# A hybrid decoder trunk on one core: priority of the norm roots, residual sums through PSUM, first weights and last block in parts, a 512-column down-projection

## The chip, the cores and the metric

The kernel runs on one core of one Trainium2 chip. The metric is the device time of one execution in microseconds (us), the median of repeated runs. TensorE multiplies, VectorE (DVE), ScalarE (ACT) and GpSimd (POOL) do the rest, SyncE (SP) issues the transfers.

## What is computed

Sixteen meta tokens stand before 1024 real ones: 1040 positions, 1024 features, float32. Two layers, each a mixer and a convolutional feed-forward network (FFN), and around each of these four a pre-norm, a post-norm and a residual:

```python
h = h + rmsnorm(mix, g[1])
ff = conv_ffn(rmsnorm(h, g[2]), ffn_w_up[l], ffn_conv[l], ffn_w_down[l])
h = h + rmsnorm(ff, g[3])
# conv_ffn: u = causal_dwconv(x @ w_up); gate, val = split(u); (silu(gate) * val) @ w_down
```

Layer 0 mixes with a gated linear recurrence over 8 heads (q, forget gate, value and output gate are projections of the normed input), layer 1 with a forgetting attention of 16 heads on shared keys and values. The output is h of the real tokens.

## The kernel before, in words

Features lie on partitions: 8 row tiles (kt) of 128 features by 1040 tokens. Tokens are cut into three blocks, 356, 342 and 342 columns in layer 0 (BLK_A), 342 each in layer 1 (BLK_B, from column 14). Every product of a weight and an activation is three matmuls on a high and a low part of each, in float32r (mm3s, L145, L148, L149). So every weight is loaded raw, cast by ACT to its high part (L97 or L135) and subtracted by DVE to its low part (L98, L138).

A norm's factor is not applied to the input but to the result. rstd_of turns a sum of squares into a factor for every column: small matmuls against ones (L164) sum over features, ACT takes the root (L169), DVE the reciprocal (L170) and a scaled diagonal (L175), matmuls spread it over all partitions in PSUM (L176), ACT copies it to SBUF where it is kept (L179). sumsq squares on ACT (L187) and adds on POOL (L188).

Layer 0's mixer begins with inputs(0): for each block four projections of head 0 (forget gate, output gate, values, queries) from weights w0, then norm0, then the four results are scaled. take(i) loads a block of x and splits it. For the later heads a hand-written order on TensorE (manual_schedule, weave) mixes the recurrence of one head with the projections of the next; for head 0 and for the post stages the order on every engine is made by a scheduler at build time, from a plan of costs and the priorities; high_priority(offset=OFF) moves instructions ahead in it. The engines then run their queues in that order and wait where something is late.

The last product before each post-norm (mixer_out's two, and the last chunk of an FFN's down-projection) runs through overlap: for each block eight output tiles, each evacuated by DVE (L575 for a mixer, L681 for an FFN) with high priority, squared and added; and, one tile into the next block, post of the block before. post calls rstd_of and then, for each row tile, loads the residual (L206), scales by gain and factor in place (L207), adds the residual (L208), stores (L210), splits the new stream for the next projections (L281 with a gain, L98 without) and adds up its squares for the next norm. With `then`, the first up-projections (or head 0 of the attention) run behind, block by block.

An FFN has 22 hidden tiles in seven chunks. For each chunk the hidden tiles are made (up-projection, convolution at L607 to L617, silu at L643, L644), then down adds the chunk's product to eight accumulators, per output tile and block, evacuated at L681. [...]

## Time and profile before

| | us |
|---|---|
| median of 3 runs | 2875.55 (2873.24 to 2882.78) |
| the profiled execution, its own time | 2883.05 |
| its span, first to last instruction | 2881.1 |

The profile shows one execution. A span's rows give busy time by engine; idle time before an instruction is put down to what released it. [...] Post stages lie at about 570 to 660, 1340 to 1425, 2070 to 2165 and 2830 to 2881 us.

### The profile page before, as it was taken

To read this page: it belongs to the slowest core of one execution; us is meant where nothing else is said; L and a number is where in the kernel's file an instruction comes from. 1 tells how busy PE (TensorE), PEld (TensorE's weight loads), DVE (VectorE), ACT (ScalarE), POOL (GpSimd) and SP (SyncE) were. 2 spreads that over 40 slices of the span, in tenths; PEclk is the share of its full clock that TensorE was granted. 3 is DMA by queue.
4 is the path that set the end of the run, shared out by engine and by line. 5 is a ranking of instruction groups with operands and counts; after the bars stand their busy time and mean duration, and the time that the engine had idled before them with its cause. 6 is when DMAs were issued, how large, how long until landed. Compare 5 with 4: busy or idle time off the path is not lost. (4 is left out here: it accounts for less than half of the span.)

```text
span 2881.1 us, 45581 instructions
## 1 busy us (share of the span) xinstructions
PE 2768.6 (96%) x17706; PEld 2709.2 (94%) x17706; DVE 1830.8 (64%) x3737; ACT 1258.2 (44%) x2421; POOL 369.6 (13%) x741
## 2 busy tenths in 40 slices
PE   8999999989999999999889999999989999999997
PEld 8999999989999999999789988898989999999997
DVE  5545445285655655566878888887684665565566
ACT  6445445455322322233566666666555232232232
POOL 2000000041100000004400000000240100010012
PEclk9999999999999999999899999999999999999999
DMA  4111111142211111112311111112242111121103
GB/s 132 30 38 30 38 40 49 37 125 62 66 38 52 45 52 38 44 52 67 92 45 45 45 45 45 45 45 93 70 124 59 45 52 52 30 65 39 52 30 113
DMA packets 202921, 163.14 MB, mean 57 GB/s; under 512 B 13984, under 2 KB 194128, under 8 KB 202704
## 3 DMA queue, kind: packets, MB, share of 16 engines
q1 hardware_dynamic: 202704, 160.23, 19.2%
q8 instruction: 138, 2.26, 0.3%
q14 instruction: 79, 0.65, 0.1%
HBM read 139.53 MB, written 20.66 MB: 56 GB/s over the span
## 5 line engine op out<-in xcount | busy, mean ns | idle before, releaser
L145 PE MATMUL pj<-x,wh 128*128 128x342 f32 (+1 forms) x2640 | 871.1, 330 | 12.6 <-DVE u L607 6.3
L149 PE MATMUL pj<-x,wl 128*128 128x342 f32 (+1 forms) x2640 | 849.3, 322 | 2.8 <-DVE wl L98 2.8
L148 PE MATMUL pj<-x,wh 128*128 128x342 f32 (+1 forms) x2640 | 849.3, 322 | 0.0
L145 PEld LDWEIGHTS pj<-x,wh 128*128 128x128 f32 x2640 | 500.8, 190 | 18.9 <-DVE u L607 7.2
L149 PEld LDWEIGHTS pj<-x,wl 128*128 128x128 f32 x2640 | 499.9, 189 | 3.1 <-DVE wl L98 3.1
L148 PEld LDWEIGHTS pj<-x,wh 128*128 128x128 f32 x2640 | 501.5, 190 | 0.1
L145 PE MATMUL g<-h,wh 128*128 128x342 f32 (+1 forms) x1056 | 339.0, 323 | 0.3
L149 PE MATMUL g<-h,wl 128*128 128x342 f32 (+1 forms) x1056 | 337.7, 321 | 0.4 <-DVE wl L138 0.4
L148 PE MATMUL g<-h,wh 128*128 128x342 f32 (+1 forms) x1008 | 323.8, 322 | 0.0
L97 ACT CAST wh<-raw 128x1024 fp32r<-128x1024 f32 x142 | 146.0, 1045 | 341.6 <-PE g L148 282.1
L145 PE MATMUL pj<-hnh,wh 128*128 128x356 f32 (+1 forms) x720 | 261.8, 364 | 9.3 <-ACT wh L97 7.0
L681 DVE TENSOR_TENSOR acc<-acc,g 128x342 f32<-128x342 f32 (+1 forms) x288 | 147.2, 511 | 193.6 <-PE g L149 193.4
L98 DVE TENSOR_TENSOR wl<-raw,wh 128x1024 fp32r<-128x1024 f32 x142 | 180.6, 1281 | 87.1 <-ACT wh L97 76.3
L149 PE MATMUL pj<-hnh,wl 128*128 128x356 f32 (+1 forms) x720 | 233.1, 324 | 0.8 <-DVE wl L98 0.8
L148 PE MATMUL pj<-hnl,wh 128*128 128x356 f32 (+1 forms) x720 | 232.8, 323 | 0.0
L612 ACT ACTIVATE y<-u,cw 128x342 f32<-128x342 f32 (+1 forms) x258 | 150.5, 584 | 182.6 <-DVE u L607 171.9
L188 POOL TENSOR_TENSOR acc<-acc,sq 128x342 f32<-128x342 f32 (+1 forms) x162 | 168.9, 1049 | 426.5 <-ACT sq L187 396.4
L613 DVE SCALAR_TENSOR_TENSOR y<-u,cw,y 128x342 f32<-128x342 f32 (+1 forms) x258 | 148.5, 576 | 111.4 <-ACT y L612 111.2
L607 DVE TENSOR_TENSOR u<-pj,r 128x342 f32<-128x342 f32 (+1 forms) x258 | 132.2, 513 | 114.1 <-PE pj L149 110.8
L145 PEld LDWEIGHTS g<-h,wh 128*128 128x128 f32 x1056 | 198.7, 189 | 2.5 <-ACT h L97 0.6
L149 PEld LDWEIGHTS g<-h,wl 128*128 128x128 f32 x1056 | 199.4, 189 | 0.6 <-DVE wl L138 0.6
L148 PEld LDWEIGHTS g<-h,wh 128*128 128x128 f32 x1008 | 190.6, 189 | 0.7 <-DVE h L98 0.2
(237 smaller groups left out, 4937.8 us busy)
## 6 DMA issues: line engine op xcount, KB each, us to landing
raw<-in_w_up_dram SPq DMA_DIRECT2D x84, 512.0 KB, 4.0
raw<-in_w_dn_dram SPq DMA_DIRECT2D x42, 512.0 KB, 4.7
raw<-in_w_in_dram SPq DMA_DIRECT2D x32, 512.0 KB, 4.1
raw<-in_kv_w_dram SPq DMA_DIRECT2D x16, 512.0 KB, 4.1
res<-h SPq DMA_DIRECT2D x44, 171.0 KB, 2.8
h<-mix SPq DMA_DIRECT2D x40, 171.0 KB, 2.2
cn<-csum SPq DMA_DIRECT2D x32, 171.0 KB, 3.6
raw<-in_w_oa_dram SPq DMA_DIRECT2D x8, 512.0 KB, 3.5
```

The source lines that it names most:

```text
L97: A.copy(hi, src)
L98: V.tensor_sub(lo, src, f(hi))
L145: PE.matmul(pt, wh, xh[:, sl], start=(j == 0), stop=False)
L148: PE.matmul(pt, wh, xl[:, sl], start=False, stop=False)
L149: PE.matmul(pt, wl, xh[:, sl], start=False, stop=(j == n - 1))
L188: eng.tensor_add(acc, acc, sq)
L607: V.tensor_mul(u[:, 2:], pt, r()[:, sl])
L612: A.activation(y, u[:, 2:], AF.Copy, scale=cw[:, j, 2:3])
L613: V.scalar_tensor_tensor(y, u[:, 1:n + 1], cw[:, j, 1:2], y, ALU.mult, ALU.add)
L681: V.tensor_add(acc_u[ot][:, sl], acc_u[ot][:, sl], pt)
```

## The change

Seven edits. The first two weights of head 0 (forget and output gate) are loaded, cast and subtracted in parts of 2, 3 and 3 row tiles (come), between the tiles of x, and their projections are interleaved; a copy of eps on ACT stands first. For head 0 TensorE's order is the written one, the norm of a block is cut in two around a projection, and the six PSUM banks of pj, g and po are taken in turn. In rstd_of root, reciprocal, diagonal and final copy get the high priority that evacuations have. In post the scaled product goes to a PSUM bank (po) and the addition reads it there. In layer 1's FFN the down-projections but the last run over two blocks of 512 columns, the last over blocks of 342, 340, 214 and 128. Before the last chunk the whole residual stream of layer 1 is fetched into eight units (h3), so post loads none. In the last chunk the eighth square is not added on POOL but goes to L164 as a second operand.

```diff
--- before.py
+++ after.py
@@ -1,4 +1,5 @@
 from contextlib import ExitStack
+from itertools import chain, zip_longest
 import concourse.bass as bass
 import concourse.tile as tile
@@ -47,6 +48,8 @@
 KSLACK, GSLACK, GLEAD, GL0, GL7 = 3000, 10000, 0.75, 0.5, 0.3
+COME = [0, 2, 5, 8]
 QR = 128
 SMB = {"u": 2, "y": 2, "sq": 2, "sq2": 1, "acc": 2, "rstd": 1, "res": 2}
 PSB = {"pj": 2, "g": 3, "pd": 2, "po": 1}
@@ -89,6 +92,8 @@
     V.memset(eps, EPS)
     gsb = cst.tile([P, 9, KT], F32, name="gsb")
     nc.sync.dma_start(gsb, gains)
+    A.copy(eps, eps)
     cw = cst.tile([P, 2 * FT - 1, 3], F32, name="cw")
     halos = cst.tile([P, 12, 2], F32, name="halos")
@@ -128,6 +133,21 @@
                 split(wh[:, :D], wl[:, :D], raw[:, :D])
             return lambda kt: (wh[:, kt * P:(kt + 1) * P], wl[:, kt * P:(kt + 1) * P])
+        def come(self, w, c0):
+            raw, wh, wl = self.load(lambda raw: [], "w")
+            def steps():
+                for a, b in zip(COME, COME[1:]):
+                    c = slice(a * P, b * P)
+                    nc.sync.dma_start(raw[:, c].rearrange("p (k c) -> p k c", c=P),
+                                      w[c, c0:c0 + P].rearrange("(k p) c -> p k c", p=P))
+                    yield
+                    split(wh[:, c], wl[:, c], raw[:, c])
+                    yield
+            return (lambda kt: (wh[:, kt * P:(kt + 1) * P], wl[:, kt * P:(kt + 1) * P])), steps()
         def rows(self, w, r0, n=P, name="w"):
             raw, wh, wl = self.load(lambda raw: [(raw[i:i + n, :D], w[r0:r0 + n, :]) for i in range(0, P, n)], name)
@@ -152,6 +172,14 @@
     def mm3(pt, pairs, sl):
         for _ in mm3s(pt, pairs, sl):
             pass
+    def whole(g):
+        while True:
+            try:
+                next(g)
+            except StopIteration as e:
+                return e.value
     def rstd_of(accs, r=None):
@@ -165,18 +193,23 @@
         q = sm.tile([P, 4], F32, tag="rq", name=nm("rq"), bufs=2)
         m = cs[-1].stop - cs[-1].start
         k = len(cs) - (m < QR)
-        for rows, j in ((QR, slice(0, k)), (m, slice(k, len(cs))))[:1 + (m < QR)]:
-            A.activation(q[:rows, j], pt[:rows, j], AF.Sqrt, bias=eps[:rows])
-            V.reciprocal(q[:rows, j], q[:rows, j])
-        dg = tmp("rstd", n)
+        with tc.high_priority(offset=OFF):
+            for rows, j in ((QR, slice(0, k)), (m, slice(k, len(cs))))[:1 + (m < QR)]:
+                A.activation(q[:rows, j], pt[:rows, j], AF.Sqrt, bias=eps[:rows])
+                V.reciprocal(q[:rows, j], q[:rows, j])
+            dg = tmp("rstd", n)
+            for j, c in enumerate(cs):
+                m = c.stop - c.start
+                V.tensor_scalar(dg[:m, c], ident[:m, :m], q[:m, j:j + 1], float(D), ALU.mult, ALU.mult)
+        yield
         pr = psum("pd")[:, :n]
         for j, c in enumerate(cs):
             m = c.stop - c.start
-            V.tensor_scalar(dg[:m, c], ident[:m, :m], q[:m, j:j + 1], float(D), ALU.mult, ALU.mult)
             PE.matmul(pr[:, c], ones[:m], dg[:m, c], start=True, stop=True)
         if r is None:
             return pr
-        A.copy(r, pr)
+        with tc.high_priority(offset=OFF):
+            A.copy(r, pr)
     def sumsq(acc, src, tag="sq", eng=G):
         if acc is None:
@@ -191,21 +224,21 @@
     def post(acc, m, sl, gpost, res, keep, pre=None, more=None):
         n = sl.stop - sl.start
-        r1 = rstd_of([acc])
+        r1 = whole(rstd_of(acc if isinstance(acc, list) else [acc]))
         acc = None
         for kt in range(KT):
             mk = m[kt][:, sl]
-            if more is None or kt % 4 < 2:
-                rs = tmp("res", n)
-            elif isinstance(more, int):
-                ru = unit(more, "res") if kt % 2 == 0 else ru
-                rs = ru[:, (kt % 2) * 350:][:, :n]
+            if isinstance(res, list):
+                rs = res[kt][:, sl]
             else:
-                rs = tmp(more[kt % 2], n)
-            nc.sync.dma_start(rs, res[kt][:, sl])
-            V.scalar_tensor_tensor(mk, mk, gsb[:, gpost, kt:kt + 1], r1, ALU.mult, ALU.mult)
-            V.tensor_add(mk, mk, rs)
+                rs = tmp(more[kt % 2] if more and kt % 4 > 1 else "res", n)
+                nc.sync.dma_start(rs, res[kt][:, sl])
+            t = psum("po")[:, :n]
+            V.scalar_tensor_tensor(t, mk, gsb[:, gpost, kt:kt + 1], r1, ALU.mult, ALU.mult)
+            V.tensor_add(mk, t, rs)
             dst = keep(kt, sl)
             nc.sync.dma_start(dst, mk[:, n - dst.shape[-1]:])
             if pre is not None:
@@ -213,7 +246,7 @@
                 acc = sumsq(acc, mk, "sq2")
         yield
         if pre is not None:
-            rstd_of([acc], pre[2][:, sl])
+            whole(rstd_of([acc], pre[2][:, sl]))
     def overlap(blocks, work, done, then=None):
@@ -290,9 +323,9 @@
     r0 = unit(45, "r0")
     hTv = hT.rearrange("(k p) t -> k p t", p=P)
     W = Weights([30, 31, 36, 37], [(24, 25), (26, 27), (28, 29), (42, 43)], OFF_W0)
-    def take(i):
+    def take(i, kts=range(KT)):
         sl = slice(BLK_A[i][0], BLK_A[i][0] + BLK_A[i][1])
-        for kt in range(KT):
+        for kt in kts:
             nc.sync.dma_start(x0[kt][:, sl], hTv[kt][:, sl])
             split_gain(hn[kt], x0[kt][:, sl], 0, kt, sl)
@@ -301,11 +334,18 @@
         accs = [None, None]
         for kt in range(KT):
             accs[kt % 2] = sumsq(accs[kt % 2], x0[kt][:, sl], eng=V if i == 0 and kt % 2 else G)
-        rstd_of(accs, r0[:, sl])
-    w0 = [W.cols(w_in, [D])]
-    take(0)
-    w0.extend(W.cols(w_in, [c * D]) for c in (3, 2, 0))
+        yield from rstd_of(accs, r0[:, sl])
+    w0 = []
+    for c in (1, 3):
+        w, g = W.come(w_in, c * D)
+        w0.append(w)
+        behind = [g] if c == 1 else behind + [g]
+    for a, b in zip(COME, COME[1:]):
+        for g in 2 * behind:
+            next(g)
+        take(0, range(a, b))
+    w0.extend(W.cols(w_in, [c * D]) for c in (2, 0))
     hg = cst.tile([P, KT], F32, name="hg")
     nc.sync.dma_start(hg, head_g)
     lb2 = cst.tile([P, 2, KT], F32, name="lb2")
@@ -416,15 +456,28 @@
         parts = [(1, forget_gate), (3, output_gate), (2, values), (0, queries)]
         if h == 0:
+            tags, done = ["pj", "pj", "g", "g", "g", "po"], [fn for _, fn in parts]
             for i, block in enumerate(BLK_A):
                 pts = []
-                for w, tag in zip(w0, ("pj", "pj", "g", "g")):
-                    yield from project(w, block, lambda *a: pts.append(a), tag)
-                norm0(i)
-                for (_, done), a in zip(parts, pts):
-                    done(*a)
+                gs = [project(w, block, lambda *a: pts.append(a), tags[(4 * i + j) % 6]) for j, w in enumerate(w0)]
+                yield from (x for xs in zip_longest(*gs[:2]) for x in xs) if i == 0 else chain(*gs[:2])
+                norm = norm0(i)
+                if i:
+                    next(norm)
+                yield from gs[2]
                 if i < len(BLK_A) - 1:
                     take(i + 1)
+                for _ in norm if i else [next(norm)]:
+                    pass
+                if i:
+                    for fn, a in zip(done, pts):
+                        fn(*a)
+                yield from gs[3]
+                for _ in norm:
+                    pass
+                for fn, a in list(zip(done, pts))[3 if i else 0:]:
+                    fn(*a)
             decays()
             keys()
             for t0, n in BLK_A:
@@ -537,8 +590,9 @@
             V.tensor_mul(o[:, sl], o[:, sl], rt[:, sl])
             yield 4 * n
-    for _ in inputs(0):
-        pass
+    with tc.manual_schedule(engines={mybir.EngineType.PE}):
+        for _ in inputs(0):
+            pass
     for h in range(HEADS - 1):
         with tc.manual_schedule(engines={mybir.EngineType.PE}):
             weave(recurrence(h), GCOL + GSLACK + KSLACK, inputs(h + 1), DCOL * GLEAD, -GL0 if h == 0 else 0.0)
@@ -594,7 +648,8 @@
     r1 = unit(40, "r1")
     keep = lambda j: lambda kt, sl: h_dram[j][kt][:, sl]
-    def ffn(l, blocks, x, r, WW, hid, accu, done, then=None):
+    def ffn(l, blocks, x, r, WW, hid, accu, done, then=None, dn=None, last=None, before=None):
         acc_u = [None] * KT
         ups = []
@@ -683,15 +738,22 @@
             def work(acc, ot, sl):
                 down(ot, sl)
                 with tc.high_priority(offset=OFF):
+                    if last and ot == KT - 1:
+                        sq = tmp("sq", sl.stop - sl.start)
+                        A.activation(sq, acc_u[ot][:, sl], AF.Square)
+                        return [acc, sq]
                     return sumsq(acc, acc_u[ot][:, sl])
             if ci == len(CHUNKS) - 1:
-                overlap(blocks, work, lambda acc, sl: done(acc, acc_u, sl), then)
+                if before:
+                    before()
+                overlap(last or blocks, work, lambda acc, sl: done(acc, acc_u, sl), then)
                 return
             for ot in range(KT):
                 if ci == 0:
                     acc_u[ot] = unit(accu[ot], f"acc{ot}")
-                for t0, n in blocks:
+                for t0, n in dn or blocks:
                     down(ot, slice(t0, t0 + n))
         count = {"hid": 0, "halo": 0}
@@ -1018,10 +1080,18 @@
     rest()
     WA = Weights([30, 31], [(37, 41), (42, 43)])
     pTh, pTl = unit(32, "pTh", F32R), unit(45, "pTl", F32R)
+    h3 = []
+    def fetch():
+        for kt, u in enumerate((0, 1, 2, 3, 8, 9, 10, 11)):
+            h3.append(unit(u, "h3"))
+            nc.sync.dma_start(h3[kt][:, B0:], h_dram[2][kt][:, B0:])
     first, rest = ffn(1, BLK_B, x3, lambda: r3, WU, [(4, 12), (5, 13), (6, 14), (7, 15)], [20, 21, 22, 23, 26, 27, 28, 29],
                       lambda acc, m, sl: post(
-                          acc, m, sl, 7, h_dram[2],
-                          lambda kt, sl: outv[kt][:, max(sl.start - NMETA, 0):sl.stop - NMETA], None, ("u", "y")))
+                          acc, m, sl, 7, h3, lambda kt, sl: outv[kt][:, max(sl.start - NMETA, 0):sl.stop - NMETA]),
+                      before=fetch, dn=[(16, 512), (528, 512)], last=[(16, 342), (358, 340), (698, 214), (912, P)])
     one, two = mixer_out(oload, w_ob, BLK_B, W, [26, 27, 28, 29, 20, 21, 22, 23],
                          lambda acc, m, sl: post(acc, m, sl, 5, h_dram[1], keep(2), (6, x3, r3)),
                          first)
```

## Rows read from the trace of the kernel before

**Rows 1.** The page, part 1: busy time and share of TensorE and the others.
```profile
PE 2768.6 (96%) x17706; PEld 2709.2 (94%) x17706; DVE 1830.8 (64%) x3737; ACT 1258.2 (44%) x2421; POOL 369.6 (13%) x741
```

**Rows 2.** The waits of PE over the span: total us, times, longest.
```profile
PE pd L164 <- POOL acc L188: 15.1, 12, 3.6
...
PE pd L176 <- DVE rstd L175: 9.7, 11, 3.1
```

**Rows 3.** Timeline, the start: start us, us, engine, line, operation [idle before <-releaser].
```profile
3.77 1.28 ACT L280 ACT_TABLE_LOAD   x1 [3.77 <-DMA x<-in_hT_dram]
...
7.02 0.66 PE L145 MATMUL pj<-hnh,wh 128*128 128x356 f32 x1 [7.02 <-ACT wh L97]
```

**Rows 4.** Timeline, PE at the end of head 0.
```profile
64.98 0.87 PE L176 MATMUL pd<-rstd,ones 128*128 128x128 f32 x6 [1.05 <-DVE rstd L175]
...
66.94 0.67 PE L145 MATMUL pj<-hnh,wh 128*128 128x356 f32 x1 [1.08 <-DVE s L366]
```

**Rows 5.** Windows behind the gaps: us, busy (instructions) by engine, PEclk, DMA, GB/s.
```profile
65.80:73.80 8.00, 6.92 (x27) 6.87 (x27) 2.40 (x6) 6.42 (x7) 0.00 (x0) 0.58 0.20 60
...
598.00:609.50 11.50, 11.44 (x50) 11.25 (x51) 4.52 (x14) 2.63 (x8) 3.72 (x5) 0.55 0.03 9
...
650.40:657.00 6.60, 4.37 (x17) 4.14 (x18) 5.93 (x11) 4.87 (x12) 4.33 (x7) 0.55 0.52 160
...
1366.90:1377.40 10.50, 10.39 (x46) 10.39 (x47) 3.98 (x13) 2.52 (x8) 2.86 (x4) 0.54 0.04 14
...
2096.40:2107.50 11.10, 11.02 (x48) 11.03 (x49) 3.11 (x12) 2.61 (x8) 3.69 (x5) 0.54 0.03 10
```

**Rows 6.** Timeline around three waits of L164 in the post stages.
```profile
584.12 2.31 POOL L188 TENSOR_TENSOR acc<-acc,sq 128x356 f32<-128x356 f32 x2 [0.30 <-ACT sq L187]
...
584.37 1.27 DVE L208 TENSOR_TENSOR mix<-mix,res 128x356 f32<-128x356 f32 x1
...
598.06 1.20 PE L164 MATMUL pd<-ones,acc 128*128 128x1 f32 x6 [2.42 <-POOL acc L188]
...
1367.01 1.18 PE L164 MATMUL pd<-ones,acc 128*128 128x1 f32 x5 [3.63 <-POOL acc L188]
...
2096.48 1.12 PE L164 MATMUL pd<-ones,acc 128*128 128x1 f32 x6 [2.57 <-POOL acc L188]
```

**Rows 7.** DVE by source line (ns min/median/max) and by form (busy us, mean ns).
```profile
L208 DVE TENSOR_TENSOR acc<-acc,res x24: 502/510/2206, 1348.3 to 2875.9; 128x342 f32<-128x342 f32 x20, 128x356 f32<-128x356 f32 x4
...
L207 DVE SCALAR_TENSOR_TENSOR mix<-mix,gsb,pd x48: 555/563/585, 576.6 to 2142.1; 128x342 f32<-128x342 f32 x40, 128x356 f32<-128x356 f32 x8
...
L681 DVE TENSOR_TENSOR acc<-acc,g 128x342 f32<-128x342 f32 x240 | 122.2, 509 | 158.5 <-PE g L149 158.2
```

**Rows 8.** Timeline, from a square root to TensorE, 638 to 655 us.
```profile
641.34 0.41 ACT L169 ACTIVATE rq<-pd,eps 128x2 f32<-128x2 f32 x2
...
645.06 0.21 DVE L170 RECIPROCAL rq<-rq 128x2 f32<-128x2 f32 x2
...
650.45 0.73 PE L176 MATMUL pd<-rstd,ones 86*128 86x86 f32 x2 [3.07 <-DVE rstd L175]
...
653.36 0.65 PE L145 MATMUL pj<-x,wh 128*128 128x342 f32 x1 [2.18 <-DVE u L607]
```

**Rows 9.** Timeline, PE: pitch of 342 columns (14 steps) and 470 (two).
```profile
2549.80 0.32 PE L148 MATMUL pj<-x,wh 128*128 128x342 f32 x1
...
2551.99 0.32 PE L145 MATMUL pj<-x,wh 128*128 128x342 f32 x1
...
1498.70 0.38 PE L879 MATMUL pd<-ks,qs 128*114 128x470 f32 x1
...
1499.13 0.21 PE L882 MATMUL pd<-maskb,identb 114*114 114x114 bf16 x1
```

**Rows 10.** Timeline, the tail.
```profile
2866.14 0.76 PE L164 MATMUL pd<-ones,acc 128*128 128x1 f32 x6 [2.36 <-POOL acc L188]
...
2869.23 1.05 DVE L207 SCALAR_TENSOR_TENSOR acc<-acc,gsb,pd 128x342 f32<-128x342 f32 x2 [1.14 <-PE pd L176]
```

## The prediction

> **What bounds the kernel now.** I read the page first. TensorE is busy for 96% of the span [rows 1], so the time can fall only where it idles, where its clock is low, or where it gets less work. Next, the waits of TensorE: the two norm steps head the list, the wait for GpSimd's last addition to a sum of squares (L164) and that for the scaled diagonal (L175 before L176), 15.1 and 9.7 us together [rows 2]. Then the timeline around the longest of them, and windows behind each. [...] At a mean clock of 0.55, 11.5 us lose 11.5 x 0.45 = 5.2 us. So a gap of 2.4 us costs almost 8 us, and a gap removed is worth three times its length. Last, VectorE's lines: in the post stages (the norm and residual after each mixer and each down-projection) it has no idle time, and what it does late is what the gaps wait for.
>
> **Start and head 0.** TensorE starts at 7.02, when one whole weight has been loaded and cast; ACT loads a table at 3.77, after the first tile of x has landed [rows 3]. The change loads two weights in parts of 2, 3 and 3 row tiles between the tiles of x, and ACT's table is loaded by a copy of eps that waits for nothing. Then the first two row tiles of each weight and one tile of x suffice, and the table's 1.28 us are gone: I put the first matmul at 5.0, a gain of 2.0. The order of TensorE is now written out. The normalisation of a block is split by a projection, so that the roots run beside 24 matmuls; at the end of head 0 this covers gaps of 1.05 and 1.08 us [rows 4], and with them the low clock from 65.8 to 73.8, 8.0 x 0.42 = 3.4 us [rows 5]. At most 2.0 + 2.1 + 3.4 = 7.5. Against it: SP issues more and smaller transfers, and in a fixed order whatever is late stops everything behind it on TensorE; the matmuls of L164 stand before the third or fourth projection and wait for the additions on GpSimd. If one block waits as long as the worst of rows 2, 3.6 us, and loses nothing in clock, the part is worth 3.9 less. From a loss of 2 to a gain of 7.5; I take **-6**, near the upper end, since the squares of a block are ready one projection ahead.
>
> **Residual sums through PSUM.** Now L207 scales in place and L208 adds the residual, both from SBUF. At 584.37 one L208 takes 1.27 us, while GpSimd works from 584.12 on [rows 6]; undisturbed it takes 0.51, at worst 2.2 [rows 7]. L207, which has one operand in PSUM, never takes more than 0.585 in 48 [rows 7]. With the product in PSUM, L208 has one SBUF operand too and should stay near the 0.51 that L681 takes with an operand in PSUM [rows 7]. An output in PSUM is shown by no DVE row; I bound it by 0.5 and 1.0 (twice L207) and take L207's own 0.56. In a block, five such additions stand in a row, so VectorE gains 5 x (1.27 - 0.51) = 3.8 us before the gap at 598.06, which is 2.42 [rows 6]. Two more places have this shape: 3.63 at 1367.01 and 2.57 at 2096.48. With the low clock behind them (5.2, 4.8 and 5.1 [rows 5]) the three hold 8.6 + 5.2 + 4.8 + 5.1 = 23.7 us.
>
> I do not take all of it. The splits behind the residual (L281, and L98 after the FFN) still read two SBUF tensors beside GpSimd, and L98 is a plain tensor_tensor like L208. And there is one PSUM bank for t, so L207 and L208 must alternate where now two of each run back to back at about 0.5 [rows 10]. I take the gaps at 598 and 2096 as halved with half of their clock, and the middle one as staying: (2.4 + 2.6 + 5.2 + 5.1) / 2 = 7.7, and 1.3 for the shorter posts elsewhere: **-9**, bounds -21 and 0.
>
> [...] The rows show an addition from PSUM as fast as one from SBUF [rows 7]. [...]
>
> **Roots ahead of the evacuations.** The square roots of a block end at 641.75 (641.34 + 0.41), but its reciprocal runs at 645.06, behind other DVE work of the post and the convolution; TensorE waits 3.07 at 650.45 and 2.18 at 653.36 for what follows [rows 8], and 6.6 x 0.45 = 3.0 us go to the clock [rows 5]. With the evacuations' priority the reciprocal and the diagonal go ahead; what they displace is some 1 us of DVE work per block. At stake are the 9.7 us of L176 [rows 2], 2.2 and 3.0. It is VectorE as a whole that is full there: what is pushed back (evacuations and conv steps) is late next, and TensorE waits for those too (653.36 is such a wait). So I take a third: **-5**, bounds -15 and +3.
>
> **Down-projection 512 wide.** In layer 1's chunks but the last there are 53 matmuls per output tile and block (8 in the first, where the half tile takes two, and 5 x 9): 8 x 53 x 3 = 1272 of 342 columns become 848 of 512. [...] The widest pair in the trace, 470 columns, takes 0.215 each [rows 9]; a line through 342 and 470 gives 0.234 for 512, and a gain of 0.5. I take **-4**. VectorE has fewer additions to make; a matmul now needs two of the earlier blocks, which are ready a block before.
>
> **Last block in parts.** After the last projection matmul (2866.14 less its wait of 2.36, 2863.8 [rows 10]) the span runs 17.3 us longer, 11.9 of them from 2869.23 on [rows 10]: eight pairs of L207 and L208 on 342 columns, a wait for residuals, the last store. With 128 columns the pairs take between 3/8 and all of their 8 us; I take 5. The residuals are fetched whole before the last chunk (eight transfers on SP, beside three blocks of matmuls, 45 us, in place of 24 loads between the stores), and the last Square goes straight to TensorE, past GpSimd's addition: 1 us each. Fewer columns in the root steps: 1. [...] Sum 3 + 2 + 1 = 6 less 2: **-4**, bounds -9 and +3.
>
> **Sum.** -6 - 9 - 5 - 4 - 4 = -28. The profiled execution took 2883.05 us (span 2881.1), 7.5 above the median of 2875.55; I make the sum on the profile and take it off the median: 2847.5, rounded 2848.
>
> **The rivals.**
> First, **contention moves on** (22%): GpSimd's additions and VectorE's splits still exclude each other, so the lost 0.76 us turn up at L281 or L98, and the gaps at 598, 1367 and 2096 stay. For it speaks that the splits follow each residual immediately; against it, that they now seldom wait. The residual part is 0, the roots -3, the rest holds: 2875.5 - 17 = 2858. [...]
>
> Second, **little arrives** (12%): the start's order gives back what it gains, the roots displace as much as they save, the wide matmuls follow the 470 row. -2, 0, 0, -0.5 and -4 make -6.5: 2869, within 0.3%.
>
> Third, **the order of TensorE at the start stalls** (10%): all three normalisations wait 3.6 us; the first part turns to +4, the rest holds: -18, 2857.
>
> Fourth, **slower** (8%): the single bank. A block of a post has eight pairs, eight evacuations of 0.51 [rows 7] and eight splits of about the same, 8.2 together; now two L207 overlap to 1.05 [rows 10], so pairs cost 0.9 and VectorE's sum is 8 x 0.9 + 8.2 = 15.4, just above the 96 x 0.156 = 15.0 that TensorE needs for a block. Run strictly end to end, with an output in the middle of its bounds (0.8), a pair costs 0.8 + 0.51 = 1.3: 18.6, 3.2 more for each of nine blocks, 29 in all. The other parts give 19 back: +10, 2886. It decides where no other ready work fills the bubble between L207 and L208, and once a pair costs more than (15.0 - 8.2) / 8 = 0.85.
>
> The forecast has 48%. A measurement of this kernel can tell about 0.3%, 8.6 us: forecast, first and third rival are faster by more (80%), the second is the same (12%), the fourth slower (8%). The range reaches from -50 (the start, the residual, the roots and the tail near their upper bounds) to the second rival: 2826 to 2870.
>
> **What would show it.** First matmul near 5; no wait of L164 over 1 us at the two mixers and full clock behind it; L208 at 0.51 everywhere; the reciprocal within 1 us of its root; wide matmuls at 0.227 to 0.234; last matmul to the end in 11 us. It is wrong if L281 or L98 grow to 1.2, if L207 exceeds 0.8, or if head 0 ends later than now.

## The result and the profile after

The changed kernel takes 2847.98 us (median of 4 runs, 2847.02 to 2849.61) against 2879.11 for the kernel before on the same chip: a ratio of 0.9895, interval 0.9882 to 0.9909. The forecast was 2848. The number was hit, but not by its terms: two of the five (the residual sums and the last block) were far off, in opposite directions. The profiled executions, 2883.05 and 2847.02 us, have spans of 2881.1 and 2845.3, and the 35.8 us between them can be divided by stage. Both kernels run the same stages, so the first and last start of a few VectorE lines are milestones.

Rows of single lines, kernel before: durations (min/median/max, ns), then first and last start in us. L575 once for each mixer, L607 once for each FFN:

```profile
L575 DVE TENSOR_TENSOR mix<-mix,pj x24: 494/510/526, 556.3 to 613.8; 128x342 f32<-128x342 f32 x16, 128x356 f32<-128x356 f32 x8
L681 DVE TENSOR_TENSOR acc<-acc,g x144: 497/511/528, 788.7 to 1385.9; 128x342 f32<-128x342 f32 x96, 128x356 f32<-128x356 f32 x48
L607 DVE TENSOR_TENSOR u<-pj,r x129: 498/514/530, 618.8 to 1324.7; 128x342 f32<-128x342 f32 x86, 128x356 f32<-128x356 f32 x43
...
L575 DVE TENSOR_TENSOR mix<-mix,pj x24: 496/510/512, 2056.0 to 2112.3; 128x342 f32<-128x342 f32 x24
L681 DVE TENSOR_TENSOR acc<-acc,g x144: 499/510/514, 2285.0 to 2863.8; 128x342 f32<-128x342 f32 x144
L607 DVE TENSOR_TENSOR u<-pj,r x129: 495/514/517, 2117.6 to 2814.7; 128x342 f32<-128x342 f32 x129
```

The same lines of the changed kernel (L575 is now L629, L681 L736, L607 L662):

```profile
L629 DVE TENSOR_TENSOR mix<-mix,pj x24: 491/511/525, 550.9 to 601.6; 128x342 f32<-128x342 f32 x16, 128x356 f32<-128x356 f32 x8
L736 DVE TENSOR_TENSOR acc<-acc,g x144: 498/512/528, 771.4 to 1360.2; 128x342 f32<-128x342 f32 x96, 128x356 f32<-128x356 f32 x48
L662 DVE TENSOR_TENSOR u<-pj,r x129: 497/514/530, 606.4 to 1307.5; 128x342 f32<-128x342 f32 x86, 128x356 f32<-128x356 f32 x43
...
L629 DVE TENSOR_TENSOR mix<-mix,pj x24: 497/511/513, 2024.2 to 2074.4; 128x342 f32<-128x342 f32 x24
L736 DVE TENSOR_TENSOR acc<-acc,g x112: 276/686/690, 2241.5 to 2833.8; 128x512 f32<-128x512 f32 x80, 128x342 f32<-128x342 f32 x8, 128x340 f32<-128x340 f32 x8, 128x214 f32<-128x214 f32 x8
L662 DVE TENSOR_TENSOR u<-pj,r x129: 499/514/517, 2079.0 to 2767.8; 128x342 f32<-128x342 f32 x129
```

From these and VectorE's first instruction on a score of the attention (L884 at 1455.8 before, L946 at 1426.8 after) come the lengths of eight stages. The table, in us, is worked out from the starts of each profiled run; all the kernels named are told of below. Each row is one execution. "Mixer A" runs from its first evacuation (L629) to the first addition of the second chunk (L736), and so holds the posts; "FFN 0" goes on to its last convolution step (L662); "posts, attention's start" to the first score; "last chunk" from the last convolution step to the end of the span.

| kernel | up to mixer A | mixer A | FFN 0 | posts, attention's start | attention | mixer B | FFN 1 | last chunk | span |
|---|---|---|---|---|---|---|---|---|---|
| before | 556.2 | 232.4 | 536.0 | 131.1 | 600.2 | 229.0 | 529.7 | 66.4 | 2881.1 |
| changed | 550.9 | 220.5 | 536.1 | 119.3 | 597.4 | 217.2 | 526.4 | 77.4 | 2845.3 |
| x1_sbuf | 549.4 | 235.6 | 536.1 | 128.6 | 598.2 | 230.1 | 526.5 | 78.0 | 2882.5 |
| x2_roots | 550.1 | 222.2 | 536.1 | 115.2 | 599.2 | 223.0 | 526.6 | 76.8 | 2849.2 |
| x3_both | 551.1 | 232.1 | 536.1 | 131.0 | 599.1 | 226.1 | 526.4 | 73.7 | 2875.5 |
| x4_last3 | 551.6 | 220.4 | 536.1 | 123.4 | 598.8 | 215.7 | 526.4 | 65.6 | 2838.1 |
| x5_dn342 | 549.5 | 220.5 | 536.1 | 121.0 | 596.0 | 218.1 | 529.4 | 77.4 | 2847.9 |
| x6_quarters | 549.7 | 220.4 | 536.1 | 119.2 | 597.7 | 215.6 | 526.5 | 64.7 | 2829.9 |
| x7_oldstart | 557.5 | 222.1 | 536.3 | 117.8 | 597.9 | 217.3 | 526.5 | 81.0 | 2856.5 |
| x8_respsum | 551.3 | 225.9 | 536.2 | 121.2 | 600.0 | 220.8 | 526.6 | 80.9 | 2862.9 |
| x9_nopool | 551.4 | 215.0 | 536.1 | 116.1 | 597.8 | 212.9 | 526.6 | 86.3 | 2842.1 |
| x9_sbuf_nopool | 550.6 | 222.5 | 536.1 | 113.2 | 595.4 | 219.8 | 526.6 | 72.1 | 2836.4 |
| x11_sumpsum | 553.6 | 225.6 | 536.1 | 121.2 | 597.8 | 224.7 | 526.7 | 66.6 | 2852.4 |
| x12_own | 551.1 | 239.8 | 536.1 | 132.1 | 598.6 | 237.9 | 526.5 | 81.2 | 2903.2 |

The changed kernel, x4_last3 and x6_quarters have, in their traces, the same instructions in the same order on every engine up to the last convolution step. Yet they differ by 4.2 us in the posts before the attention (119.2 to 123.4), by 1.9 up to mixer A and by 1.6 in mixer B. A difference of that size between two rows can't be put down to an edit.

So the change took 5.3 us off the start, 11.9, 11.8 and 11.8 off the three stages with posts, 2.8 off attention and 3.3 off FFN 1, and it put 11.0 on the last chunk. In the waits of TensorE the two heads of [rows 2] fell: that for the scaled diagonal from 9.7 us to 7.5 (first row), that for the sum of squares from 15.1 to 6.6 (last row). One rose, from 4.2 in all and 3.3 at most: the wait for VectorE's work on the first scores, which stands at the end of the stage before the attention (second row).

```profile
PE pd L208 <- DVE rstd L203: 7.5, 12, 2.9
PE pd L941 <- DVE c L946: 7.5, 3, 6.6
...
PE pd L192 <- POOL acc L221: 6.6, 12, 1.0
```

The window over the first mixer's posts (columns: length, busy time of PE, PEld, DVE, ACT, POOL, then the granted clock, 1.00 being full, DMA share, GB/s) has full clock, where [rows 5] showed 0.55 twice. Half clock stands here for stretches that read 0.50 to 0.58. The second row is the last chunk, where part of it now sits, and the third the stage from FFN 0's last convolution step to the first score, where part of it stayed (before, 0.89 over 131.1 us):

```profile
550.00:700.00 150.00, 144.77 (x906) 139.98 (x905) 102.25 (x199) 80.32 (x161) 56.62 (x74) 1.00 0.34 96
...
2812.00:2833.60 21.60, 20.25 (x145) 19.96 (x145) 11.82 (x36) 4.67 (x15) 5.95 (x11) 0.82 0.19 66
...
1307.50:1426.80 119.30, 105.12 (x642) 100.34 (x640) 91.99 (x181) 69.65 (x145) 54.90 (x50) 0.94 0.35 103
```

### The profile page after: what moved, and what is told of

The parts are those of the page before. It is cut to its first block, busy times and chain, and to the rows that moved or that the text cites. A ratio compares the mean times of both kernels' runs of the same rounds, so it can differ in the third digit from the quotient of the medians.

```text
span 2845.3 us, 44989 instructions
## 1 busy us (share of the span) xinstructions
PE 2758.4 (97%) x17396; PEld 2662.5 (94%) x17396; DVE 1816.0 (64%) x3726; ACT 1257.2 (44%) x2425; POOL 367.3 (13%) x744
## 5 line engine op out<-in xcount | busy, mean ns | idle before, releaser
L165 PE MATMUL g<-h,wh 128*128 128x342 f32 (+5 forms) x944 | 322.1, 344 | 3.9 <-DVE acc L736 3.4
L169 PE MATMUL g<-h,wl 128*128 128x342 f32 (+5 forms) x944 | 320.9, 342 | 0.0
L168 PE MATMUL g<-h,wh 128*128 128x342 f32 (+5 forms) x904 | 307.7, 342 | 0.0
L102 ACT CAST wh<-raw 128x1024 fp32r<-128x1024 f32 (+2 forms) x146 | 146.8, 1022 | 339.1 <-PE g L168 285.4
L736 DVE TENSOR_TENSOR acc<-acc,g 128x342 f32<-128x342 f32 (+5 forms) x256 | 141.7, 556 | 202.6 <-PE g L169 202.6
L165 PE MATMUL pj<-hnh,wh 128*128 128x356 f32 (+1 forms) x704 | 255.4, 363 | 6.9 <-ACT hnh L313 5.7
L103 DVE TENSOR_TENSOR wl<-raw,wh 128x1024 fp32r<-128x1024 f32 (+2 forms) x146 | 178.5, 1231 | 86.5 <-ACT wh L102 80.2
L169 PE MATMUL pj<-hnh,wl 128*128 128x356 f32 (+1 forms) x704 | 226.6, 322 | 0.0
L221 POOL TENSOR_TENSOR acc<-acc,sq 128x342 f32<-128x342 f32 (+4 forms) x165 | 163.1, 998 | 426.9 <-ACT sq L220 401.3
L662 DVE TENSOR_TENSOR u<-pj,r 128x342 f32<-128x342 f32 (+1 forms) x258 | 132.5, 514 | 115.6 <-PE pj L169 110.1
L165 PEld LDWEIGHTS g<-h,wh 128*128 128x128 f32 x944 | 178.8, 190 | 19.4 <-DVE acc L736 4.0
L169 PEld LDWEIGHTS g<-h,wl 128*128 128x128 f32 x944 | 179.4, 190 | 12.1
L168 PEld LDWEIGHTS g<-h,wh 128*128 128x128 f32 x904 | 172.0, 190 | 13.6 <-DVE h L103 1.9
```

Of the source, the lines that this page charges most:

```text
L102: A.copy(hi, src)
L103: V.tensor_sub(lo, src, f(hi))
L165: PE.matmul(pt, wh, xh[:, sl], start=(j == 0), stop=False)
L168: PE.matmul(pt, wh, xl[:, sl], start=False, stop=False)
L169: PE.matmul(pt, wl, xh[:, sl], start=False, stop=(j == n - 1))
L221: eng.tensor_add(acc, acc, sq)
```

## The experiments

All are the changed kernel with one thing different. In each, the kernel before was run on the same chip; the ratios are against it. To compare with the change, hold them against its 0.9895. The line numbers shift by up to three between kernels, in x7_oldstart by 22.

**x1_sbuf: the product back in SBUF.**

```diff
-            t = psum("po")[:, :n]
-            V.scalar_tensor_tensor(t, mk, gsb[:, gpost, kt:kt + 1], r1, ALU.mult, ALU.mult)
-            V.tensor_add(mk, t, rs)
+            V.scalar_tensor_tensor(mk, mk, gsb[:, gpost, kt:kt + 1], r1, ALU.mult, ALU.mult)
+            V.tensor_add(mk, mk, rs)
```

> The changed kernel with one part undone: the scaled product of a post goes back into its SBUF tile, so that the residual addition has two SBUF operands again; all else as changed (2848 us). By stages the changed kernel gained 5.4 us at the start, 11.9, 11.7 and 11.7 at the three places with posts, 2.7 in attention and 3.4 in layer 1's feed-forward, and lost 11 in the last chunk; the 38 us of posts and attention are to be shared between this part and the roots' priority. Theory (contention, as in the prediction, but mis-sized): the addition is back at 0.62 us on average with single ones over 1.2 us beside GpSimd, VectorE is late again, and gaps over 2 us with the half clock behind them come back at least at one mixer: 2858 to 2875. Rival (the roots' priority did it): the additions are longer, but the gaps stay closed: 2846 to 2853. Second rival (the single PSUM bank costs something): faster than 2846.

Measured: 2881.87 us, ratio 1.0010 (1.0001 to 1.0018). The whole gain is gone, more than any of the three expected. The first mixer's posts show how. VectorE in this kernel, in order of time (start, duration):

```profile
579.61 0.57 DVE L313 SCALAR_TENSOR_TENSOR x<-mix,gsb,x 128x356 fp32r<-128x356 f32 x1
580.11 1.28 DVE L240 TENSOR_TENSOR mix<-mix,res 128x356 f32<-128x356 f32 x1
581.32 0.57 DVE L239 SCALAR_TENSOR_TENSOR mix<-mix,gsb,pd 128x356 f32<-128x356 f32 x1
581.81 0.50 DVE L628 TENSOR_TENSOR mix<-mix,pj 128x342 f32<-128x342 f32 x1
582.23 0.58 DVE L313 SCALAR_TENSOR_TENSOR x<-mix,gsb,x 128x356 fp32r<-128x356 f32 x1
582.73 1.28 DVE L240 TENSOR_TENSOR mix<-mix,res 128x356 f32<-128x356 f32 x1
```

GpSimd beside it, and VectorE and GpSimd of the changed kernel in the same place:

```profile
579.87 2.31 POOL L221 TENSOR_TENSOR acc<-acc,sq 128x356 f32<-128x356 f32 x2 [0.30 <-ACT sq L220]
582.49 2.32 POOL L221 TENSOR_TENSOR acc<-acc,sq 128x356 f32<-128x356 f32 x2 [0.31 <-ACT sq L220]
```

```profile
580.98 0.52 DVE L241 TENSOR_TENSOR mix<-po,res 128x356 f32<-128x356 f32 x1
581.53 0.59 DVE L240 SCALAR_TENSOR_TENSOR po<-mix,gsb,pd 128x356 f32<-128x356 f32 x1
582.03 0.51 DVE L629 TENSOR_TENSOR mix<-mix,pj 128x342 f32<-128x342 f32 x1
582.45 0.71 DVE L314 SCALAR_TENSOR_TENSOR x<-mix,gsb,x 128x356 fp32r<-128x356 f32 x1
583.08 0.52 DVE L241 TENSOR_TENSOR mix<-po,res 128x356 f32<-128x356 f32 x1
```

```profile
579.73 6.36 POOL L221 TENSOR_TENSOR acc<-acc,sq 128x342 f32<-128x342 f32 x6 [0.27 <-ACT sq L220]
```

With two SBUF operands each of the five additions from 577.49 on falls into one of GpSimd's and takes 1.28 or 1.29 us, and the four instructions of a row tile repeat every 2.62 us (580.11 to 582.73). From PSUM the addition takes 0.52 beside a GpSimd that works without a break, and the period is 2.10 (580.98 to 583.08); the mean of the six tiles from 573.73 to 587.04 is 2.22, since some splits are slow. TensorE needs 1.9 us for a row tile (12 products of 0.156 [rows 9]). So the stage is paced by VectorE at 2.62, and close to TensorE's own pace at 2.1 to 2.2. The waits for the sum of squares come back, and with them two of 5 to 6 us for a convolution's first step, longer than any such wait before the change (2.2):

```profile
PE pd L192 <- POOL acc L221: 15.4, 10, 3.6
...
PE pj L165 <- DVE u L661: 11.0, 2, 5.9
```

**x2_roots and x3_both: no priority for the roots, with and without the bank.**

```diff
-        with tc.high_priority(offset=OFF):
+        if True:
             for rows, j in ((QR, slice(0, k)), (m, slice(k, len(cs))))[:1 + (m < QR)]:
...
-        with tc.high_priority(offset=OFF):
+        if True:
             A.copy(r, pr)
```

> The changed kernel with the priority of the square roots, reciprocals, scaled diagonals and of the copy of r taken away, all else as changed (2848 us). Theory (the prediction's shares, 9 to the residual and 5 to the roots, scaled to the 38 us found): the reciprocal runs some 3 us after its root again, TensorE waits for the scaled diagonal 9 to 10 us in all instead of 7.5, and 10 to 15 us are lost: 2858 to 2863. Rival (the priority did most of it): 20 us or more are lost, 2868 or above, with the half clock behind the mixers' norm steps again. Second rival (what it displaces costs as much): 2845 to 2851.

> Both of the two undone at once: the product in SBUF and no priority for the roots; start, wide down-projection and parts of the last block as changed. If the ledger by stages is right and these two parts alone made the 38 us of the posts and of attention, the three stages with posts are as long as before the change: 2848 + 35 to 38 = 2883 to 2886. If the start's order or other tiles' places moved the posts by themselves, less: 2865 to 2878. With the two single runs it tells whether the parts add up (x1's loss + x2's loss = this loss), help only together (each alone loses nearly all of it) or stand in for one another (each alone loses little).

Measured: x2 2851.40 us, ratio 0.9911 (0.9898 to 0.9924), 3.4 us above the changed kernel, with overlapping intervals: just beyond the second rival's range and well short of the theory's 10 to 15 us. x3 2880.55, 1.0009 (0.9998 to 1.0020), is not to be told from x1. The waits for the diagonal rise to 12.2 us in x2, more than the 9 to 10 expected. By stages 5.8 us are lost at mixer B, and the 4.1 won in FFN 0's posts are no more than identical code shows. So the priority is worth some 3 us, not clear of noise, and nothing can be seen of it without the bank; whether the parts add up (34 and 3 alone, 33 together) can't be told. The table also says which part carries the gain: from mixer A to mixer B, FFN 0 left out, x2 (the bank alone) is 33 us shorter than the kernel before, x3 (neither) 4.

**x4_last3: the last chunk in three blocks.**

```diff
-dn=[(16, 512), (528, 512)], last=[(16, 342), (358, 340), (698, 214), (912, P)])
+dn=[(16, 512), (528, 512)], last=[(16, 342), (358, 340), (698, 342)])
```

> The changed kernel with the last chunk in blocks of 342, 340 and 342 columns instead of 342, 340, 214 and 128; the residuals are fetched whole and the last Square goes past GpSimd as changed. Theory (a matmul of 214 or of 128 columns takes the same 0.111 us, as long as the weight load beside it): 96 x (2 x 0.111 - 0.156) = 6.3 us of TensorE come off, and the 2.65 us gap before a 214-column product and the 3.3 us that the half clock behind it costs go too, while the post after the last matmul has 342 instead of 128 columns, 8 x (0.58 + 0.51 - 0.72) = 3 us longer, and roots in three columns: 2848 - 12 + 3 = 2839, between 2836 and 2842. Rival (the 11 us that the last chunk grew by come from the residuals' transfers or from the Square's new place): 2846 to 2851. Second rival (the shorter tail was worth its matmuls): 2850 or more.

Measured: 2841.79 us, ratio 0.9878 (0.9865 to 0.9890): 6.2 us faster than the changed kernel, with intervals that overlap. The last chunk, the one stage whose code differs, is 11.8 us shorter (77.4 to 65.6), the expected 9 and more. In the profiled executions 4.1 us of it are lost in FFN 0's posts, though every engine has the same instructions there in the same order: there a wait of 3.6 us for a sum of squares, which the changed kernel's profile does not have, ends at 1384, and x6_quarters has it too (3.3). Why it comes in one execution and not in another is open.

```profile
PE pd L192 <- POOL acc L221: 10.2, 13, 3.6
```

In the changed kernel's last chunk, products of 214 columns at full clock, then after a gap in the low clock, then products of 128 at either:

```profile
2805.25 0.28 PE L165 MATMUL g<-h,wh 128*128 128x214 f32 x1
2805.36 0.27 PE L168 MATMUL g<-h,wh 128*128 128x214 f32 x1
2805.47 0.28 PE L169 MATMUL g<-h,wl 128*128 128x214 f32 x1
...
2812.11 0.55 PE L165 MATMUL g<-h,wh 128*128 128x214 f32 x1 [2.65 <-DVE acc L736]
...
2813.09 0.41 PE L168 MATMUL g<-h,wh 128*128 128x214 f32 x1
2813.31 0.41 PE L169 MATMUL g<-h,wl 128*128 128x214 f32 x1
...
2825.06 0.28 PE L169 MATMUL g<-h,wl 128*128 128x128 f32 x1
2825.17 0.28 PE L165 MATMUL g<-h,wh 128*128 128x128 f32 x1
...
2833.13 0.41 PE L168 MATMUL g<-h,wh 128*128 128x128 f32 x1
2833.35 0.41 PE L169 MATMUL g<-h,wl 128*128 128x128 f32 x1
```

Both widths start every 0.11 us at full clock and every 0.21 to 0.22 at half, though one has 1.7 times the columns of the other. In x4 the 96 products of a block of 342 take 15 us as before, and no gap or low clock is left ahead of the last of them:

```profile
2772.60:2820.00 47.40, 47.40 (x316) 47.39 (x315) 30.47 (x68) 13.64 (x29) 15.86 (x18) 1.00 0.33 124
```

**x6_quarters: four blocks of 256.** The same edit with `last=[(16, 256), (272, 256), (528, 256), (784, 256)]`.

> The changed kernel with the last chunk in four blocks of 256 columns instead of 342, 340, 214 and 128. Parts of 214 and 128 columns had one pitch, 0.111 us; three blocks made the last chunk 12 us shorter. Theory (a floor of 0.111 us under every product, which 256 columns pass just above): a pitch of about 0.121, 4 x 96 x 0.121 = 46.4 us of TensorE, 1.2 more than the three blocks, and a tail of 256 columns instead of 342, some 1.4 us shorter: the last chunk takes 64 to 68 us from the last convolution to the end, where the parts took 77.5 and three blocks 65.5; in all 2836 to 2846. Rival (four blocks instead of three cost it, by their posts and waits): 72 us or more for that stretch, 2846 or above.

Measured: 2842.90 us (2831.59 to 2847.89), ratio 0.9872 (0.9850 to 0.9893), the last chunk 64.7 us. Four blocks cost nothing that shows; narrow ones do. The pitch, from ten steps, is (2776.11 - 2774.92) / 10 = 0.119, just under the 0.121 expected:

```profile
2774.92 0.28 PE L165 MATMUL g<-h,wh 128*128 128x256 f32 x1
...
2776.11 0.28 PE L168 MATMUL g<-h,wh 128*128 128x256 f32 x1
```

The three-block and the quartered kernel have the lowest medians of the kernels that leave nothing out; their intervals overlap the change's a little, and they are not to be told apart. The profiled execution of x6 (2831.59) is the fastest of its four, 11 us below their median, so its row in the table flatters it.

**x5_dn342: the down-projection back to 342 columns.** The edit leaves `dn` away.

> The changed kernel with layer 1's down-projections in blocks of 342 columns again instead of 512 (the parts of the last block stay). From the first addition of the second chunk to the last convolution of layer 1 the kernel before took 529.7 us and every kernel with wide blocks so far 526.4 to 526.6. Theory (the pitch: 3 x 0.1564 - 2 x the pitch of a 512-column product): the stretch is back at 529.5 to 530, and the whole at 2848 + 3.4 = 2851, between 2848 and 2855 since the order of other stages can shift a few us either way. Rival (VectorE's fewer additions or the reach over two blocks made the 3.3): the stretch is back, but with waits of TensorE for the additions in it, which the wide kernel does not have. Second rival (something else shortened it): the stretch stays at 526.5.

Measured: 2852.50 us, ratio 0.9911 (0.9896 to 0.9927), as the theory had it, FFN 1 back at 529.4. Neither kernel has a wait of TensorE in that stretch, so the pitch is all of it.

**x7_oldstart: the start of before.** The edit puts the old lines of w0, take, norm0 and inputs(0) back, without the copy of eps and without the written order.

> The changed kernel with the start of before: one whole weight and then the first block of x, no copy of eps, each normalisation after its four projections, TensorE's order left to the scheduler. Theory (the ledger by stages: 5.4 us ahead when head 0 is done, and unchanged from there to the first mixer): 2848 + 5 = 2853, between 2851 and 2856, first matmul at 7.0, a gap of 1 us or more and the half clock behind it at the end of head 0. Rival (the lead is lost in the weave of the heads, whose order is fixed by hand): 2846 to 2850.

Measured: 2858.47 us, ratio 0.9935 (0.9920 to 0.9950): 10.5 lost where 5 were expected. The start itself costs 6.6 (557.5 against 550.9), the first matmul comes at 7.42. Another 3.6 are in the last chunk, whose code is the same: there the low clock lasted longer (0.63 from 2820 to 2847 us). Parts of 214 and 128 columns make that stretch uncertain: 77.4, 77.4 and 81.0 us with the same code (changed, x5, x7), 72.1 to 86.3 over all the kernels in the table that have them, whose posts differ. The two ends, after a 214-column gap, are x9_nopool at a mean clock of 0.53 over 31 us,

```profile
2800.00:2831.00 31.00, 30.32 (x146) 29.88 (x146) 12.48 (x38) 4.57 (x15) 0.00 (x0) 0.53 0.13 46
```

and x9_sbuf_nopool, at 0.93 from 2800 to 2826; the changed kernel's 0.82, shown above, lies between.

**x8_respsum: the residual through the bank instead of the product.**

```diff
             t = psum("po")[:, :n]
-            V.scalar_tensor_tensor(t, mk, gsb[:, gpost, kt:kt + 1], r1, ALU.mult, ALU.mult)
-            V.tensor_add(mk, t, rs)
+            A.copy(t, rs)
+            V.scalar_tensor_tensor(mk, mk, gsb[:, gpost, kt:kt + 1], r1, ALU.mult, ALU.mult)
+            V.tensor_add(mk, mk, t)
```

> The changed kernel with the roles in a post's addition swapped: the scaled product goes back into its SBUF tile, in place, and the residual is copied by ACT into the PSUM bank that held the product, so the addition again has one operand in SBUF and one in PSUM, while nothing of VectorE is written to PSUM. Undoing the PSUM part alone cost 34 us (2881.9 against 2848). Theory (what counts is that the addition does not read two SBUF tensors beside GpSimd): the addition stays at 0.51 us, never over 0.7, and the time near the changed kernel's, 2846 to 2858, ACT's 96 more copies of some 0.45 us costing a little. Rival (what counts is the product's way into a bank of its own, which sets the order of products and additions): the additions are short, but the gaps at the mixers come back, 2870 to 2885.

Measured: 2858.43 us, ratio 0.9938 (0.9920 to 0.9956), just past the upper edge of what the theory gave (2858), and far from the rival's 2870. No mixer addition exceeds 0.524 us. Most of the gain stays (23 of 34 us) although the product is in place in SBUF: the operand's place matters.

**x9_nopool and x9_sbuf_nopool: without seven eighths of GpSimd's additions, from PSUM and in SBUF.** Both leave the sums of squares incomplete.

```diff
+            if add:
                 eng.tensor_add(acc, acc, sq)
...
-                acc = sumsq(acc, mk, "sq2")
+                acc = sumsq(acc, mk, "sq2", add=kt == KT - 1)
```

> The changed kernel without seven eighths of GpSimd's additions: in the sums of squares of the mixers, down-projections and posts only the last of a block is made (so the norms' values are not those of the reference; the squares are still made, and TensorE still waits for one addition); the first norm keeps all of its additions. It is the partner of the next run. Theory (contention): what is left of it, 8 splits over 0.8 us in the first mixer's posts alone, goes: 2835 to 2845. Rival (VectorE is not what bounds the posts any more): 2846 to 2850.

> The same additions of GpSimd left out, and the product of a post in its SBUF tile as before the change, so the residual addition has two SBUF operands, but hardly a GpSimd instruction beside it. With GpSimd working, SBUF instead of PSUM cost 34 us. Theory (the collision of two-SBUF additions with GpSimd's is the cause): no addition over 0.7 us, and within 4 us of its partner above, 2835 to 2849. Rival (the order or the bank is the cause, GpSimd a bystander): 25 to 35 us above its partner, 2862 to 2880.

Measured: 2839.24 us (ratio 0.9864, 0.9847 to 0.9880) and 2838.76 (0.9867, 0.9852 to 0.9882). With GpSimd at work the bank is worth 34 us, without it nothing in total: the theory's number. The table tempers this. The SBUF kernel's last chunk is 14.2 us shorter, 2 of it behind the last product and the rest by the half clock shown above; its two mixers are still 7.5 and 6.9 longer, by two waits,

```profile
PE pj L165 <- DVE u L662: 9.8, 2, 5.2
```

for a convolution's first step that stands in VectorE's queue behind products and additions. With GpSimd the mixers lost 15.1 and 12.9 without the bank, and the posts before the attention 9.3; so, by these single executions, about half of the mixers' loss and all of the posts' is the collision, and the rest of the mixers' is something else, perhaps that one bank keeps products from being put ahead of their additions.

**x12_own: the product in one SBUF buffer of its own,** to separate the two.

```diff
-SMB = {"u": 2, "y": 2, "sq": 2, "sq2": 1, "acc": 2, "rstd": 1, "res": 2}
+SMB = {"u": 2, "y": 2, "sq": 2, "t": 1, "acc": 2, "rstd": 1, "res": 2}
...
-            t = psum("po")[:, :n]
+            t = tmp("t", n)
...
-                acc = sumsq(acc, mk, "sq2")
+                acc = sumsq(acc, mk)
```

> The changed kernel with the scaled product of a post in one SBUF buffer of its own instead of the one PSUM bank (room for it is made by letting a post's squares use the two buffers of the other squares). It separates the two things that the bank does. In place in SBUF, the two stretches with mixers took 235.6 and 230.1 us against 220.5 and 217.3 with the bank; without GpSimd's additions they took 222.5 and 219.8 against 215.0 and 212.9, with two waits of 5 us for a convolution's first step, which stood in VectorE's queue behind products and additions that had been put ahead of it. Theory (two halves: the collision with GpSimd, and the single buffer, which keeps products from being put ahead of their additions): additions over 1.2 us are back, but no wait over 3 us for the convolution's first step at the two mixers; they take 226 to 230 and 222 to 226, and the whole 2862 to 2876. First rival (the collision is all of it): as in place, 234 us or more at the first mixer, 2878 or above. Second rival (the single buffer is all of it): as with the bank, 219 to 222, 2846 to 2852.

Measured: 2904.00 us, ratio 1.0082 (1.0068 to 1.0096). By its numbers this is the first rival's (2878 or above, 239.8 us at the first mixer), but far above where the product in place came out (2881.87). Additions of 1.28 are back and the long waits for the convolution's step are not, as the theory had it; but the room was made by sharing the squares' buffers, and the longest wait now is again the one for the sum of squares, 6.3 us at most where x1 had 3.6:

```profile
PE pd L192 <- POOL acc L221: 24.3, 13, 6.3
```

That the sharing made it longer is likely, not shown. So the first rival can't be credited either: the kernel doesn't settle how the mixers' loss divides. That stays open.

**x11_sumpsum: the sum in PSUM too, with x4's last chunk.**

```diff
+            mixer = gpost in (1, 5)
+            t = psum("g" if mixer else "po")[:, :n]
...
+            V.tensor_add(t if mixer else mk, t, rs)
+            if mixer:
+                A.copy(mk, t)
...
+                split_gain(pre[1][kt], t if mixer else mk, pre[0], kt, sl)
```

> The last chunk in three blocks, as in x4 (2841.8 us), and in the two mixers' posts the residual sum itself stays in PSUM, in the three banks that the down-projections use and that idle there: ACT copies it to SBUF for the store, and the split reads it from PSUM, so that none of VectorE's three instructions of a row tile reads two SBUF tensors. Theory (the rest of the contention sits in the splits, 8 of 24 over 0.8 us in the first mixer): no split over 0.7 us there, and each mixer's stretch (220.5 and 217 us from its first addition to the second chunk's first) is 3 to 6 us shorter, about as far as without GpSimd's additions (215 and 213): 2830 to 2837. Rival (ACT's 48 more copies take its place): splits short, stretches as long or longer, as with the residuals copied by ACT (226 and 221): 2842 to 2852.

Measured: 2854.12 us, ratio 0.9913 (0.9900 to 0.9927), 12 above x4 and 2 above the rival's range. The splits are short (first row), but ACT makes 48 more copies, waiting for the sum (second row), and the mixers are 5.2 and 9.0 us longer than x4's. So the rival's outcome came: what is left of the collision costs less than moving it in this way.

```profile
L317 DVE SCALAR_TENSOR_TENSOR x<-g,gsb,x 128x342 fp32r<-128x342 f32 x40 | 22.7, 567 | 3.1 <-ACT x L316 2.9
```

```profile
L244 ACT COPY mix<-g 128x342 f32<-128x342 f32 x40 | 17.6, 439 | 14.6 <-DVE g L242 14.6
...
PE pj L165 <- DVE u L665: 9.4, 4, 4.3
```

That ACT's copies are the reason is not shown. The product has three banks here in place of one, and two waits of 4.3 us for a convolution's first step are back (third row), one in each mixer. Such waits reach 5 to 6 us with the product in place in x1_sbuf and x9_sbuf_nopool, though only 2.3 in x8_respsum and 2.6 in x3_both, and at most 2.1 with the product in a single bank or buffer (changed, x2_roots, x12_own). That leans towards the guess that a single one keeps products from being put ahead, but no run changes the number of buffers alone.

## Why the prediction was right in its number and wrong in two terms

**Start, -6: right.** 5.3 us by the stages, 6.6 by x7. The first matmul starts at 5.67, not 5.0; the gaps at the end of head 0 [rows 4] and the low clock behind them are gone (1.00 from 65 to 73 us, where [rows 5] had 0.58). The third rival, a stalling order, did not come.

**Residual sums, -9 with a bound of -21: mis-sized.** Undoing them costs 34 us. The step that failed is "I do not take all of it", the halving of the gaps with half of their clock, and the middle gap "as staying". In the profiled execution all three waits for L221's sum are at most 1.0 us, and the low clock behind the mixers is gone ([rows 5] had 0.55 for 11.5 us at the first and 0.54 for 11.1 at the second; now 596 to 607 and 2060 to 2080 read 1.00). In the middle stage a wait of 2.9 us for the diagonal is left at 1369.8, with a clock of 0.83 over the 10 us behind it, and one of 6.6 us before the third of the first scores; x4 and x6, with the same code there, still have a wait of over 3 us for the sum. The reason given, that the splits still collide, came true without the consequence: in the first mixer's posts 8 of 24 splits take over 0.8 us (one did before), and the mean over both mixers rose from 635 to 728 ns for 342 columns, and single splits reach the 1.2 us that the prediction named as a sign of being wrong (1.29, but 1.22 before the change as well). Yet a row tile's period fell to 2.22 us on average. The test was the period against TensorE's 1.9. The prediction worked out that pair only in its fourth rival, for the changed kernel and with undisturbed splits; for this term it summed a block's additions (5 x 0.76) ahead of one gap. The bound was too tight as well, since it counted three gaps and not the waits behind them [rows 8].

**First rival, contention moves on (22%):** half true, as just told; its time, 2858, would have needed the gaps to stay. **Fourth rival, the single bank:** the product takes 0.57 us into PSUM, 0.595 at most, so a pair costs about 1.1 with the gap between; but L629 and L314 fill that gap, and the mixers got shorter. Where nothing fills it, the price shows: in the tail a pair of 128 columns takes 0.72 us (additions at 2837.29 and 2838.00) against 0.46 in x1_sbuf (two in 0.92), 2 us over eight. With x12_own's one SBUF buffer it is 0.71, so the price is that of a single buffer and not of PSUM. An addition from PSUM took no longer than one from SBUF: a median of 0.504 us at the mixers in place of 0.513. Beside GpSimd's additions it took 0.52 from PSUM and 1.28 from SBUF; by what means GpSimd holds it up is not shown.

**Roots, -5: the right order of size, 3.4,** but not clear of noise. That VectorE as a whole is full, so that what is displaced is late next, was the right caution, though "no idle time" was too strong: it is busy 75.8 of the 90 us from 570 to 660 of the kernel before.

**Down-projection, -4: right,** 3.3 by the stages and 3.0 by x5. The 512-column pitch is 0.230 us (20 steps, 2441.22 to 2445.82), under the 0.234 of the line through [rows 9], which alone gives a gain of 0.5. The rest of the 4, and the lower end of the 0.227 to 0.234 named as the test, took part of a product's time as fixed whatever its width; no run shows that part.

**Last block, -4: wrong sign, +11.0.** The failing step is the "less 2", for 96 added matmuls and a post beside them. The matmuls' part of it was worked out from the same fixed part of a product, which no run shows, and no row had been read at 214 or 128 columns. Measured, both widths cost 0.111 each: 96 x (0.222 - 0.156) = 6.3 us. In 12 x 0.111 = 1.3 us per output tile, VectorE's pair of product and addition (1.1) and its evacuation (0.37) no longer fit. Between two evacuations, at 2807.44 and 2811.68, it runs four products and three additions, and TensorE waits 2.65 us for the second one, until 2812.11, with the half clock behind it. The tail did shorten, from 17.3 to 11.5 us between the last product and the end, against 11 forecast.

**The sum.** -28 was forecast; the profiled pair shows -36, the medians on one chip -31. Terms missed by -24 (residuals and roots, with the attention) and +15 (last block) partly cancelled, and taking the sum off the low median of 2875.55 did the rest. A hit like this confirms no term.

## What to carry to other kernels

Where an engine stage paces TensorE, work out its period per tile from the rows, contended instructions included, and hold it against TensorE's period: here the gain came nearly whole once the period was near enough, though the contention had in part only moved. Before a block is cut to shorten a tail, read the pitch at the new width: a product of 128 columns cost here no less than one of 214 (0.111 us each). And divide the difference by stage before believing a total, but hold each stage against what identical code shows: 4 us here between two executions of one instruction order, and up to 14 in a last chunk at half clock.

## What was not expected of the hardware

In layer 1's FFN, where every product has a weight load of its own, the pitch was 0.111 us for both 214 and 128 columns, 0.119 for 256, 0.156 for 342 and 0.230 for 512, and about 0.213 for both narrow widths at half clock. The loads beside the 214-column products started every 0.11 us too (2805.04, 2805.15, 2805.26), each recorded with 0.19. Whether the load sets the pitch there is not shown: no run took it away.

Writing a product to PSUM cost VectorE next to nothing: 0.57 us into PSUM, 0.56 into SBUF. And in a last chunk with parts of 214 and 128 columns a low clock that had come could stay: a mean of 0.53 for 31 us in x9_nopool, of 0.82 for 22 in the changed kernel. The three blocks of x4_last3 ran at 1.00 over 47.4 us, the four of x6_quarters over 48.8.
